# Four-tile column groups, sine tables on ScalarE and GpSimd roots in a two-part transformer kernel

## The chip, the cores and the metric

One core of a Trainium2 chip runs the whole program. The metric is device microseconds from start to end of one execution; lower is better. The kernel before takes 1556.37 us, the median of three runs (1552.61 to 1558.96).

## What is computed

A trunk of two layers works on 256 tokens and 256 context tokens of width 1024. Each layer has an attention branch (MLA), a pooling branch and a gated linear attention branch (GLA), which are gated, merged, multiplied with an output matrix, normalised and added to the stream. A second block follows: an RWKV-7 branch and a diagonal state-space branch (S5) in parallel, merged in the same way, and a gated feed-forward part. The lines that matter here, cut:

```python
def rmsnorm(x, g):
    y = xf * lax.rsqrt(jnp.mean(xf * xf, axis=-1, keepdims=True) + NORM_EPS)
...
def s5_branch(u, ...):
    a_bar = jnp.exp(lam * dt)                 # lam complex: modulus and phase
    bu = einsum('gpc,blgc->blgp', b_bar, ug)
    _, states = associative_scan(s5_combine, (a_elems, bu), axis=1)
    y = real(einsum('gcp,blgp->blgc', c, states)) + d * ug
...
def gla_inputs(zz, af_w2, af_b, ab_w2, ab_b):
    log_a_f = log_sigmoid(zz['gla_af'] @ af_w2 + af_b) / GLA_TAU
```

## The kernel before, in words

Activations lie with channels on the 128 partitions and tokens along the columns. SBUF holds an arena of 62 slots of 128x512 float32 (`S.get`, `S.put`; the oldest free slot is given out first). Weights come as units of 1 MB on SyncE's queue into raw tiles; `split` (L424, L426) makes a rounded high part on ScalarE and a low part on VectorE, or on GpSimd for each fourth one, and `mm3` (L441) does three matmuls per block of weights. A compile-time scheduler orders each engine's instructions by the order in which the program is written, as far as its own model finds them ready; on the chip each engine then runs its list in order. `weave` alternates the steps of a chain with those of a filler.

`rsqrt` (L488 to L496) computes a reciprocal root of a 128 x n tile in nine VectorE instructions: a first guess by integer arithmetic and two refinements. n is 2 at the boundaries between stages, 4 in `mla_prep`, 2 or 4 at the end of a GLA head, and 16 in two places of RWKV. `bcast` (L468) spreads the n columns over the partitions by TensorE transposes. `boundary` takes two roots in sequence: `r` normalises the output that has just been collected, and the root of `new` (L565) normalises the updated stream, of which `enter` then builds the next stage's input. For each of the eight channel tiles `update_x` adds the output to the stream, on GpSimd (L649, L650) or on VectorE (L653, L654, issued behind the second root), and `build_h` (L634 and the lines after it) makes high and low parts; the first matmuls of the next stage (`pen`) follow tile by tile.

`s5_prepare` runs woven with the third branch merge of layer 0. It computes sine and cosine of 32 phases per state row on ScalarE, and then, for each of 16 tiles, a table of 256 cosines and 256 sines by the addition theorem: six GpSimd products and sums (L1443 to L1448), stored to DRAM on SyncE's queue. In this stage `lo_every` keeps the low parts of the weights off GpSimd. `s5_chain` later loads a table per tile i, forms the inputs (`bu`, L1575), turns them (L1578 to L1581), scans (`recur`), and `output(i)` multiplies with C: four float32 matmuls of 32 columns of weights by 256 columns, which add up in rows 32(i mod 4) of one PSUM bank (L1559, tile `py`; two hardware records each).

`gla_decay` makes four gate matmuls with 32 rows of weights (L1026). The RWKV chain works in 64x64 quadrants: `sc`/`scl` (L1759, L1761), `pw` (L1815: eight heads of the upper half, then eight of the lower), `prh` (L1834: four of one half, then four of the other), `pmn` (L1849, L1850), `pyo` (L1856, L1857). `pQ`, `pY` and `pX` alternate the halves already.

Of the kernel before, what the change touches and what calls it, by code (L numbers as in the profile page):

```python
# [18 lines left out]
P = 128  # L19
L = 256  # L20
D = 1024
# [10 lines left out]
MOD_AT = (0, 1, 4)  # L32
S5_EARLY = (7, 5)
# [52 lines left out]
def _constants():  # L86
# [25 lines left out]
    c.add("iota", np.broadcast_to(np.concatenate([16.0 * np.arange(16), np.arange(16)]).astype(np.float32), (P, 32)))  # L112
    c.add("zero", np.zeros((P, 1), np.float32))
# [57 lines left out]
def _win_cols(w, name, t):  # L171
    if name == "misc":
        kr = w[:, OFF["kr"]:OFF["kr"] + 32]
        z = np.zeros((D, 32), w.dtype)
        return np.concatenate([kr, kr[:, ROPE_PERM], w[:, OFF["af"]:OFF["af"] + 32], z], 1)
    o = OFF[name] + P * t
    return w[:, o:o + P]
# [112 lines left out]
def gate_weights(inp, l):  # L290

    gw = np.zeros((32, 4, 2, 64), np.float32)
    gw[:16, :, 0] = np.asarray(inp["gla_af_w2"][l]).reshape(16, 4, 64)
    gw[16:, :, 1] = np.asarray(inp["gla_ab_w2"][l]).reshape(16, 4, 64)
    return _pad_rows(gw.reshape(32, 512), 64)
# [63 lines left out]
class B:  # L359
# [122 lines left out]
    def rsqrt(self, m, n):  # L482

        nc = self.nc
        r = self.sm.tile([P, 16], F32, tag="r", name="r")[:, :n]
        t = self.sm.tile([P, 16], F32, tag="t", name="t")[:, :n]
# [9 lines left out]
        self.chain_end = nc.vector.scalar_tensor_tensor(r, u, -0.9375, r, ALU.add, ALU.mult)  # L496
# [147 lines left out]
def update_x(b, k, st, xs, s_, pr, rs, on_pool):  # L644
# [26 lines left out]
def trunk(b, l, xs, st, A):  # L671
# [23 lines left out]
    if st is None:  # L695
# [13 lines left out]
        pr2 = b.bcast(b.rsqrt(A, 4), 4, b.pb)  # L709
# [312 lines left out]
    def gla_decay():  # L1022
        es = []
        for hd in range(4):
            ps = b.pa.tile([P, 512], F32, tag="p", name="pgate")
            nc.tensor.matmul(ps, gw[64:96, hd * P:(hd + 1) * P], misc[64:96], start=True, stop=True)  # L1026
# [324 lines left out]
def s5_prepare(b):  # L1351
# [29 lines left out]
    sn, cs = S.get(), S.get()  # L1381
    for t, ph in ((sn, 0.0), (cs, 0.25)):
        if ph:
            nc.vector.tensor_scalar(m, m, ph, None, ALU.add)
        nc.vector.tensor_scalar(r, m, MAGIC, -MAGIC, ALU.add, ALU.add)
        nc.vector.tensor_sub(t, m, r)
    zero = b.after((sn, cs), 0.0)
    for t in (sn, cs):
        nc.scalar.activation(t, t, AF.Sin, bias=zero, scale=6.283184)
    S.put(m, r)  # L1390
    yield
    sn3, cs3 = (t.rearrange("p (a c) -> p a c", c=32) for t in (sn, cs))

    s1, c1 = sn3[:, :, 17], cs3[:, :, 17]
# [40 lines left out]
    ring = [(S.get(), S.get()) for _ in range(2)]  # L1435
    for i in range(16):
        tab, tp = ring[i % 2]
        a3 = lambda t: t.rearrange("p (a c) -> p a c", c=16)
        can = cs[:, i * 32:i * 32 + 16].unsqueeze(2).broadcast_to((P, 16, 16))
        san = sn[:, i * 32:i * 32 + 16].unsqueeze(2).broadcast_to((P, 16, 16))  # L1440
        cbn = cs[:, i * 32 + 16:i * 32 + 32].unsqueeze(1).broadcast_to((P, 16, 16))
        sbn = sn[:, i * 32 + 16:i * 32 + 32].unsqueeze(1).broadcast_to((P, 16, 16))
# [8 lines left out]
        b.s5["tab"].append(d)  # L1451
        yield
    S.put(sn, cs, *ring[0], *ring[1])


def second_block(b, xs, st, A):
# [74 lines left out]
    def s5_chain():  # L1531
# [20 lines left out]
        def output(i):  # L1552
            _, t1, t2 = parts[i]
            rows, cc_ = slice(32 * (i % 4), 32 * (i % 4) + 32), slice(32 * i, 32 * i + 32)
            if i % 4 == 0:
                pys.append(b.pb.tile([P, 512], F32, tag="p", name="py5"))
            for n, (w_, x_) in enumerate(((cre, t1[:, 0:256]), (cren, t1[:, 256:512]), (cimn, t2[:, 0:256]),
                                          (cimn, t2[:, 256:512]))):
                nc.tensor.matmul(pys[-1][rows, C], w_[:, cc_], x_, start=n == 0, stop=n == 3)  # L1559
            S.put(t1, t2)  # L1560
# [4 lines left out]

        for i in range(16):
# [18 lines left out]
            if i > 1:  # L1585
                output(i - 2)
            yield
        recur(15)
        output(14)
        output(15)  # L1590
# [38 lines left out]
    def rwkv_chain():  # L1629
# [32 lines left out]
        rn = b.rsqrt(m16, 16)  # L1662
# [83 lines left out]
        for bt in range(2):  # L1746
            Lm, Y, X_ = S.get(), S.get(), S.get()
            for hd in range(4 * bt, 4 * bt + 4):
# [5 lines left out]
                for cc in range(2):  # L1754
                    for cp in range(2):
                        t0 = cc * P + cp * CH
                        orow = slice(cp * CH, cp * CH + CH)
                        for n, src in enumerate((BT, KT)):
                            nc.tensor.matmul(ps[orow, cc * 256 + n * P:cc * 256 + n * P + P].rearrange("p (a t) -> p a t", a=2),  # L1759
# [349 lines left out]
```

## Time and profile before

| | us |
|---|---|
| median of three runs | 1556.37 |
| the profiled execution | 1556.99 |
| its span, first to last instruction | 1555.2 |
| TensorE busy | 1435.6 |
| VectorE busy | 1101.0 |
| ScalarE busy | 688.8 |
| GpSimd busy | 491.1 |

The mean granted TensorE clock is 0.954 of full speed. A busy TensorE counts the latency of each matmul, so it is not TensorE at its peak: how close matmuls start to each other is read from the number of records in a stretch.

### The profile page before, as it was taken

The numbers are of one execution on the slowest core, as the hardware profiler recorded it, in microseconds if no ns is written. First come the engines' busy times: TensorE is split into PE (matmuls) and PEld (weight loads), VectorE is DVE, ScalarE is ACT, GpSimd is POOL, SyncE is SP. The second block draws the span as 40 slices with busy tenths as digits, with TensorE's granted clock in tenths as the row PEclk, the third lists the DMA queues.
The fourth block names the chain that finished last, engine by engine and source line by source line (L and its number), as shares of the span: only waits on it lengthen the run. The fifth ranks groups of instructions, "written<-read, shape, count | busy, mean of one in ns | idle before, by whom it ended". The sixth has DMA issues, their size and how long they took to land. (4 is left out here: it accounts for less than half of the span.)

```text
span 1555.2 us, 27544 instructions
## 1 busy us (share of the span) xinstructions
PE 1435.6 (92%) x10700; PEld 1216.2 (78%) x10700; DVE 1101.0 (71%) x2215; ACT 688.8 (44%) x1279; POOL 491.1 (32%) x503
## 2 busy tenths in 40 slices
PE   5999999998999999899998889979899999699996
PEld 1676776876788878886877789968668999699996
DVE  4565567887779555865579977768988549798843
ACT  3434445443433334454554455633532435376642
POOL 1000003354336954510035331334543003421212
PEclk8999999999999999899989999979999999799998
DMA  9534431321224253334024236734231325266560
GB/s 355 192 106 155 127 128 33 94 66 55 67 88 124 82 209 103 96 109 163 14 82 122 77 115 177 258 127 129 78 95 37 95 64 169 69 196 185 177 189 28
DMA packets 61043, 187.92 MB, mean 121 GB/s; under 512 B 7024, under 2 KB 8560, under 8 KB 60912
## 3 DMA queue, kind: packets, MB, share of 16 engines
q1 hardware_dynamic: 60912, 186.16, 38.2%
q8 instruction: 84, 1.38, 0.4%
q14 instruction: 47, 0.39, 0.1%
HBM read 180.10 MB, written 6.03 MB: 120 GB/s over the span
## 5 line engine op out<-in xcount | busy, mean ns | idle before, releaser
L424 ACT CAST wh<-raw 128x1024 fp32r<-128x1024 f32 (+1 forms) x296 | 279.5, 949 | 281.0 <-PE y L441 55.7
L426 DVE TENSOR_TENSOR wl<-raw,wh 128x1024 fp32r<-128x1024 f32 (+1 forms) x225 | 266.2, 1185 | 170.0 <-ACT wh L424 166.6
L426 POOL TENSOR_TENSOR wl<-raw,wh 128x1024 fp32r<-128x1024 f32 (+1 forms) x71 | 144.7, 2038 | 616.1 <-ACT wh L424 584.1
L441 PE MATMUL z_merge<-s,wh 128*128 128x512 f32 (+1 forms) x768 | 200.6, 351 | 1.8 <-ACT s L939 1.8
L441 PEld LDWEIGHTS z_merge<-s,wh 128*128 128x128 f32 x768 | 136.1, 198 | 19.7 <-ACT s L939 2.4
L441 PE MATMUL z_merge<-s,wl 128*128 128x512 f32 (+1 forms) x384 | 133.6, 348 | 0.3 <-DVE wl L426 0.2
L441 PE MATMUL pbr<-s,wh 128*128 128x256 f32 (+1 forms) x512 | 120.1, 326 | 0.8 <-DVE s L432 0.7
L441 PE MATMUL pup<-s,wh 128*128 128x256 f32 x656 | 118.5, 283 | 0.1
L441 PEld LDWEIGHTS pup<-s,wh 128*128 128x128 f32 x656 | 102.5, 192 | 0.2 <-ACT wh L424 0.2
L441 PE MATMUL y<-s,wh 128*128 128x256 f32 x496 | 98.1, 294 | 0.0
L441 PE MATMUL pwo<-s,wh 128*128 128x256 f32 (+1 forms) x448 | 94.1, 307 | 3.8 <-ACT s L1247 3.1
L441 PEld LDWEIGHTS pbr<-s,wh 128*128 128x128 f32 x512 | 86.8, 192 | 9.8 <-DVE s L432 1.0
L441 PE MATMUL pup<-s,wl 128*128 128x256 f32 x328 | 92.8, 283 | 0.0
L441 PEld LDWEIGHTS y<-s,wh 128*128 128x128 f32 x496 | 78.6, 193 | 7.8 <-issue 4.8
L441 PEld LDWEIGHTS z_merge<-s,wl 128*128 128x128 f32 x384 | 76.1, 198 | 9.5 <-DVE wl L426 1.1
L441 PE MATMUL pbr<-s,wl 128*128 128x256 f32 (+1 forms) x256 | 83.1, 325 | 0.0
L441 PEld LDWEIGHTS pwo<-s,wh 128*128 128x128 f32 x448 | 75.0, 199 | 7.7 <-ACT s L1247 3.7
L1134 ACT ACTIVATE s<-s 128x512 f32<-128x512 f32 (+1 forms) x64 | 33.2, 523 | 89.9 <-DVE s L1133 75.2
L441 PE MATMUL y<-s,wl 128*128 128x256 f32 x248 | 71.3, 287 | 0.0
L441 PE MATMUL pwo<-s,wl 128*128 128x256 f32 (+1 forms) x224 | 68.4, 306 | 1.5 <-DVE wl L426 1.5
L431 ACT CAST s<-s 128x256 fp32r<-128x256 f32 (+1 forms) x88 | 42.6, 488 | 60.7 <-DVE s L1204 17.9
L441 PE MATMUL pdn<-s,wh 128*128 128x256 f32 x352 | 63.4, 283 | 0.0
(480 smaller groups left out, 3618.8 us busy)
## 6 DMA issues: line engine op xcount, KB each, us to landing
raw<-wts SPq DMA_DIRECT2D x294, 512.0 KB, 4.4
s<-wts SPq DMA_DIRECT2D x57, 256.0 KB, 5.4
s5t<-s SPq DMA_DIRECT2D x16, 256.0 KB, 2.0
s<-s5t SPq DMA_DIRECT2D x16, 256.0 KB, 3.2
s<-xc SPq DMA_DIRECT2D x8, 256.0 KB, 5.0
x<-xc SPq DMA_DIRECT2D x8, 256.0 KB, 5.1
s<-tabs SPq DMA_DIRECT2D x4, 256.0 KB, 4.5
out<-s SPq DMA_DIRECT2D x8, 128.0 KB, 1.8
```

Of the source, the lines that this page charges most:

```text
L424: self.nc.scalar.copy(hi[:, :n], src)
L426: self.last_lo = eng.tensor_sub(lo[:, :n], src, hi[:, :n])
L431: self.nc.scalar.copy(hi, src)
L441: self.nc.tensor.matmul(ps, u, v[:, cols], start=start and n == 0, stop=stop and n == last)
L1134: nc.scalar.activation(E[:, lo:], E[:, lo:], AF.Exp, scale=1.0 / TAU)
```

## The change

1. `rsqrt` becomes one GpSimd instruction, the power -0.5, in 21 of 24 places; the first root of the program (n = 4) and the two roots of 16 columns keep the nine VectorE steps (`steps=True`). `update_x`'s GpSimd part is now the one that is issued behind the second root, and VectorE's part is free.
2. The 16 tables are made of phases: VectorE adds two phases (two additions of 256 columns), rounds (512 columns) and subtracts (512 columns); after each fourth tile ScalarE takes four sines of 512 columns, and four stores follow. `lo_every` and `NSLOT` stay.
3. `output` takes groups of tiles, 4, 4, 2, 2, 2 and 2, and goes round the group's column groups with each of the four terms. The group (0 to 3) is issued at step 5, the next at step 9, the pairs at 11, 13, 15 and the end; the slots of its products are held until then.
4. `gla_decay` issues its four gate matmuls as two pairs on different groups of 32 rows, and the weights are laid out twice for that. In RWKV, `sc`, `pw`, `prh`, `pmn` and `pyo` alternate halves from one matmul to the next.

```diff
-    def rsqrt(self, m, n):
+    def rsqrt(self, m, n, steps=False):
...
+        if not steps:
+            self.chain_end = nc.gpsimd.tensor_tensor(r, m, self.c("mhalf")[:, :n], ALU.pow)
+            return r
...
     if on_pool:
-        nc.gpsimd.tensor_mul(o_.ap, o_.ap, rs.ap)
-        nc.gpsimd.tensor_add(xs[s_][k], xs[s_][k], o_.ap)
+        with b.tc.issue_after(b.chain_end.ins):
+            nc.gpsimd.tensor_mul(o_.ap, o_.ap, rs.ap)
+            nc.gpsimd.tensor_add(xs[s_][k], xs[s_][k], o_.ap)
     else:
-        with b.tc.issue_after(b.chain_end.ins):
-            nc.vector.tensor_mul(o_.ap, o_.ap, pr[:, 0:256])
-            nc.vector.tensor_add(xs[s_][k], xs[s_][k], o_.ap)
+        nc.vector.tensor_mul(o_.ap, o_.ap, pr[:, 0:256])
+        nc.vector.tensor_add(xs[s_][k], xs[s_][k], o_.ap)
...
         for hd in range(4):
-            ps = b.pa.tile([P, 512], F32, tag="p", name="pgate")
-            nc.tensor.matmul(ps, gw[64:96, hd * P:(hd + 1) * P], misc[64:96], start=True, stop=True)
+            if hd % 2 == 0:
+                pgs = [b.pa.tile([P, 512], F32, tag="p", name="pgate") for _ in range(2)]
+                for i, ps in enumerate(pgs):
+                    rr = slice(64 + 32 * i, 96 + 32 * i)
+                    nc.tensor.matmul(ps, gw[rr, (hd + i) * P:(hd + i + 1) * P], misc[rr], start=True, stop=True)
+            ps = pgs[hd % 2]
...
     for i in range(16):
-        nc.gpsimd.tensor_tensor(a3(tab[:, 0:256]), can, cbn, ALU.mult)
-        nc.gpsimd.tensor_tensor(a3(tp[:, 0:256]), san, sbn, ALU.mult)
-        nc.gpsimd.tensor_tensor(a3(tab[:, 256:512]), san, cbn, ALU.mult)
-        nc.gpsimd.tensor_tensor(a3(tp[:, 256:512]), can, sbn, ALU.mult)
-        nc.gpsimd.tensor_sub(tab[:, 0:256], tab[:, 0:256], tp[:, 0:256])
-        nc.gpsimd.tensor_add(tab[:, 256:512], tab[:, 256:512], tp[:, 256:512])
-        d = b.tc.dram_tile([P, 512], F32, name=f"s5t{i}")
-        nc.sync.dma_start(d, tab)
+        for e in range(2):
+            am = mc[:, 256 * (1 - e) + 16 * i:256 * (1 - e) + 16 * i + 16].unsqueeze(2).broadcast_to((P, 16, 16))
+            bm = m3[:, i, 16:32].unsqueeze(1).broadcast_to((P, 16, 16))
+            nc.vector.tensor_tensor(t4[:, e], am, bm, ALU.add)
+        nc.vector.tensor_scalar(rd, tab, MAGIC, -MAGIC, ALU.add, ALU.add)
+        nc.vector.tensor_sub(tab, tab, rd)
+        if i % 4 == 3:
+            zero = b.after(tabs, 0.0)
+            for j, t in enumerate(tabs):
+                nc.scalar.activation(t, t, AF.Sin, bias=zero, scale=6.283184)
+                d = b.tc.dram_tile([P, 512], F32, name=f"s5t{i - 3 + j}")
+                nc.sync.dma_start(d, t)
...
-        def output(i):
+        def output(group):
+            for n, (w_, k, e) in enumerate(((cre, 1, 0), (cren, 1, 1), (cimn, 2, 0), (cimn, 2, 1))):
+                for i in group:
+                    rows, cc_ = slice(32 * (i % 4), 32 * (i % 4) + 32), slice(32 * i, 32 * i + 32)
+                    nc.tensor.matmul(pys[-1][rows, C], w_[:, cc_], parts[i][k][:, 256 * e:256 * e + 256],
+                                     start=n == 0, stop=n == 3)
...
-            if i > 1:
-                output(i - 2)
+            if i - 2 == groups[0][-1]:
+                output(groups.popleft())
...
-            for cp in range(2):
-                rr = slice(cp * CH, cp * CH + CH)
-                for hd in range(8):
+            for hd in range(8):
+                for cp in range(2):
+                    rr = slice(cp * CH, cp * CH + CH)
```

## Rows read from the trace of the kernel before

**Rows 1.** The page's first part: busy us, share of the span, instructions of each engine.

```profile
PE 1435.6 (92%) x10700; PEld 1216.2 (78%) x10700; DVE 1101.0 (71%) x2215; ACT 688.8 (44%) x1279; POOL 491.1 (32%) x503
```

**Rows 2.** Busy time by stretch; each line's columns: PE, PEld, DVE, ACT, POOL, PEclk, DMA, GB/s.

```profile
500.00:576.00 76.00, 73.98 (x316) 59.84 (x315) 43.44 (x47) 24.48 (x36) 62.00 (x76) 0.98 0.37 121
...
1047.00:1091.00 44.00, 41.40 (x284) 34.64 (x282) 37.18 (x58) 16.57 (x26) 19.91 (x15) 0.92 0.47 146
1091.00:1142.00 51.00, 46.09 (x315) 34.55 (x315) 48.09 (x74) 27.62 (x52) 33.57 (x31) 0.93 0.24 71
...
1168.00:1213.00 45.00, 44.78 (x840) 37.26 (x837) 36.90 (x57) 10.21 (x20) 15.37 (x14) 1.00 0.15 41
...
1227.00:1270.00 43.00, 43.00 (x613) 40.05 (x611) 16.11 (x45) 14.71 (x35) 2.58 (x2) 1.00 0.31 92
...
1331.00:1349.00 18.00, 7.11 (x29) 6.20 (x30) 11.93 (x38) 2.21 (x6) 8.45 (x13) 0.55 0.25 79
```

**Rows 3.** Groups of instructions: count, busy us, mean ns, idle before and its releasers.

```profile
L468 PE MATMUL ps_rb<-cons,r 128*128 128x128 f32 x60 | 12.9, 318 | 23.2 <-DVE r L496 23.2
...
L494 DVE TENSOR_SCALAR u<-t 128x2 f32<-128x2 f32 (+2 forms) x24 | 8.8, 366 | 0.7
...
L489 DVE TENSOR_TENSOR t<-r 128x2 f32<-128x2 f32 (+2 forms) x24 | 4.5, 187 | 0.5
```

**Rows 4.** Timeline, boundary ahead of the feed-forward part: start, duration, operation, [idle before <-releaser].

```profile
1339.91 0.16 DVE L561 TENSOR_TENSOR bs<-ps_ss,part 128x4 f32<-128x4 f32 x1 [1.69 <-PE ps_ss L460]
...
1341.94 0.16 DVE L565 TENSOR_TENSOR bA<-bA,bt 128x2 f32<-128x2 f32 x1
...
1342.61 0.72 POOL L649 TENSOR_TENSOR s<-s 128x256 f32<-128x256 f32 x1 [9.11 <-ACT s L662]
...
1343.39 0.65 DVE L492 TENSOR_TENSOR t<-r 128x2 f32<-128x2 f32 x1
...
1346.90 0.66 PE L468 MATMUL ps_rb<-cons,r 128*128 128x128 f32 x2 [4.77 <-DVE r L496]
1347.68 0.87 DVE L634 SCALAR_TENSOR_TENSOR s<-x,vec_b,ps_rb 128x256 f32<-128x256 f32 x2 [0.26 <-PE ps_rb L468]
...
1348.65 0.58 PE L441 MATMUL pen<-s,wh 128*128 128x256 f32 x1 [1.09 <-ACT s L636]
```

**Rows 5.** Groups of GpSimd's instructions by shape, one of the smallest and the largest.

```profile
L426 POOL TENSOR_TENSOR wl<-raw,wh 128x1024 fp32r<-128x1024 f32 x44 | 109.0, 2478 | 450.9 <-ACT wh L424 433.5 <-DMA x<-xc 17.3
...
L978 POOL TENSOR_TENSOR s<-s,cons 128x4 f32<-128x4 f32 x2 | 0.4, 202 | 0.1
```

**Rows 6.** Timeline of matmuls: start, duration of the whole batch, count; and one load group.

```profile
242.71 1.98 PE L1026 MATMUL pgate<-s,s 32*128 32x512 f32 x4
...
702.18 1.92 PE L605 MATMUL pmod<-raw,sc 128*32 128x512 f32 x16
...
1190.78 1.15 PE L1792 MATMUL pY<-s,s 64*64 64x64 f32 x32
...
1192.79 1.91 PE L1559 MATMUL py<-s,s 128*32 128x256 f32 x8
...
1226.44 1.85 PE L1815 MATMUL pw<-s,s 64*64 64x64 f32 x32
...
L1559 PEld LDWEIGHTS py<-s,s 128*32 128x32 f32 x128 | 13.5, 118 | 15.5 <-issue 5.4 <-POOL s L1581 0.7 <-DVE s L1764 0.6
```

**Rows 7.** Timeline around the phase tables, and the longest wait behind a load, 500 to 576.

```profile
467.08 0.43 DVE L1377 TENSOR_SCALAR s<-s 128x512 f32<-128x512 f32 x1
467.55 0.69 DVE L1378 TENSOR_TENSOR s<-s,s 128x512 f32<-128x512 f32 x1
...
472.72 1.28 ACT L1389 ACT_TABLE_LOAD   x1
...
584.95 0.42 DVE L519 TENSOR_TENSOR s<-s,s 128x256 f32<-128x256 f32 x1
...
ACT wh L424 <- DMA raw<-wts: 24.6, 6, 7.3
```

More of the change, by code (lines that the diff above doesn't have):

```diff
@@ L32 @@
 MOD_AT = (0, 1, 4)
+S5_GROUPS = ((4, 0), (4, 4), (2, 8), (2, 10), (2, 12), (2, 14))
 S5_EARLY = (7, 5)
@@ L112, in _constants @@
     c.add("iota", np.broadcast_to(np.concatenate([16.0 * np.arange(16), np.arange(16)]).astype(np.float32), (P, 32)))
+    c.add("mhalf", np.full((P, 16), -0.5, np.float32))
     c.add("zero", np.zeros((P, 1), np.float32))
@@ L708, in trunk @@
         nc.vector.tensor_scalar(A, ps[:, :4], EPS, None, ALU.add)
-        pr2 = b.bcast(b.rsqrt(A, 4), 4, b.pb)
+        pr2 = b.bcast(b.rsqrt(A, 4, True), 4, b.pb)
     if st:
@@ L1380, in s5_prepare @@
     nc.vector.tensor_add(m, m, r)
[L1381 to L1388, printed above, removed]
+    nc.vector.tensor_scalar(r, m, MAGIC, -MAGIC, ALU.add, ALU.add)
+    nc.vector.tensor_sub(m, m, r)
+    S.put(r)
+    mc = S.get()
+    s1, c1 = sm("s1"), sm("c1")
+    nc.vector.tensor_copy(s1, m3[:, :, 17])
+    nc.vector.tensor_scalar(c1, s1, 0.25, None, ALU.add)
+    nc.vector.tensor_scalar(k, c1, MAGIC, -MAGIC, ALU.add, ALU.add)
+    nc.vector.tensor_sub(c1, c1, k)
+    zero = b.after((s1, c1), 0.0)
+    for t in (s1, c1):
         nc.scalar.activation(t, t, AF.Sin, bias=zero, scale=6.283184)
-    S.put(m, r)
     yield
-    sn3, cs3 = (t.rearrange("p (a c) -> p a c", c=32) for t in (sn, cs))
-    s1, c1 = sn3[:, :, 17], cs3[:, :, 17]
     ur, ui, n2, kr, ki = sm("ur"), sm("ui"), sm("n2"), sm("kr"), sm("ki")
@@ L1550, in recur @@
             S.put(g5, tab)
-        def output(i):
-            _, t1, t2 = parts[i]
-            rows, cc_ = slice(32 * (i % 4), 32 * (i % 4) + 32), slice(32 * i, 32 * i + 32)
-            if i % 4 == 0:
+        def output(group):
+            if group[0] % 4 == 0:
                 pys.append(b.pb.tile([P, 512], F32, tag="p", name="py5"))
[L1557 to L1560, printed above, removed]
+            for n, (w_, k, e) in enumerate(((cre, 1, 0), (cren, 1, 1), (cimn, 2, 0), (cimn, 2, 1))):
[3 more added lines that the diff above has]
+                                     start=n == 0, stop=n == 3)
+            for i in group:
+                S.put(*parts[i][1:])
+            i = group[-1]
             if i % 4 == 3:
@@ L1564, in output @@
                 nc.scalar.activation(u_.ap, u_.ap, AF.Gelu_apprx_tanh)
+        groups = deque(range(o, o + n) for n, o in S5_GROUPS)
         for i in range(16):
@@ L1584, in s5_chain @@
                 recur(i - 1)
-            if i > 1:
-                output(i - 2)
+            if i - 2 == groups[0][-1]:
+                output(groups.popleft())
             yield
         recur(15)
-        output(14)
-        output(15)
+        for g in groups:
+            output(g)
         S.put(*s5w, sbr, sbi)
@@ L1661, in rwkv_chain @@
         nc.vector.tensor_scalar(m16, nk[:, 0:16], 1e-24, None, ALU.max)
-        rn = b.rsqrt(m16, 16)
+        rn = b.rsqrt(m16, 16, True)
         rnk = b.sm.tile([P, 16], F32, tag="rnk", name="rnk")
@@ L1754, in rwkv_chain @@
                 for cc in range(2):
+                    for n, src in enumerate((BT, KT)):
+                        for cp in range(2):
+                            t0 = cc * P + cp * CH
+                            orow = slice(cp * CH, cp * CH + CH)
+                            nc.tensor.matmul(ps[orow, cc * 256 + n * P:cc * 256 + n * P + P].rearrange("p (a t) -> p a t", a=2),
+                                             src[q].ap[rows, t0:t0 + CH], ar3[rows, :, t0:t0 + CH], start=True, stop=True)
                     for cp in range(2):
@@ L1829, in rwkv_chain @@
             if c:
-                for e in range(2):
-                    rows = slice(64 * e, 64 * e + 64)
-                    prh = b.pa.tile([P, 512], F32, tag="p", name="prh")
-                    for q in range(4):
+                prhs = [b.pa.tile([P, 512], F32, tag="p", name="prh") for _ in range(2)]
+                for q in range(4):
+                    for e, prh in enumerate(prhs):
+                        rows = slice(64 * e, 64 * e + 64)
                         nc.tensor.matmul(prh[rr, q * 64:q * 64 + 64], AR[q][rows, t0:t0 + CH], M[rows, q * 64:q * 64 + 64],
                                          start=True, stop=True)
+                for e, prh in enumerate(prhs):
                     nc.vector.tensor_add(w4[rr, :, e], w4[rr, :, e], prh[rr, 0:256].rearrange("p (q i) -> p q i", i=64))
@@ L1893, in rwkv_chain @@
         nc.vector.tensor_scalar(m16, nk[:, 0:16], 1.0 / 64, 64e-5, ALU.mult, ALU.add)
-        rn = b.rsqrt(m16, 16)
+        rn = b.rsqrt(m16, 16, True)
         rnk = b.sm.tile([P, 16], F32, tag="rnk", name="rnk2")
```

58 lines of the change are left out of this document (31 added, 27 removed).

## The prediction, made before the changed kernel ran

> **What bounds the kernel now.** I read the busy times first: TensorE 92% of the span, VectorE 71%, ScalarE 44%, GpSimd 32% [rows 1]. So most stretches end when TensorE's list ends, and an edit pays where it shortens TensorE's list or a wait ahead of it. The table of stretches [rows 2] sorts the places that the change touches. In 500 to 576 (tables woven into the merge) TensorE is busy 73.98 of 76 us, VectorE 43.44 and GpSimd 62.00: TensorE bounds, and VectorE has 32.6 us to spare. In 1047 to 1091 TensorE leads VectorE by 41.40 to 37.18 of 44. In 1091 to 1142 VectorE leads, 48.09 of 51. In 1168 to 1213 and 1227 to 1270 TensorE is busy to the last 0.2 us. In 1331 to 1349 it is busy 7.11 of 18 at a granted clock of 0.55, which is near the lower of its two levels (1.2 of 2.4 GHz): nothing bounds there but a chain of short steps. Third, the groups of instructions [rows 3]: before `ps_rb` TensorE stands idle 23.2 us, all for the last line of `rsqrt`. That is the largest wait that the change attacks. Its nine lines lie between 0.187 and 0.366 us each, some 0.27 in the mean, so 24 roots occupy VectorE for about 24 x 9 x 0.27 = 58 us. Last, the timeline of a boundary [rows 4], the one place where each step of the chain is seen.
>
> **1. Roots on GpSimd.** At the boundary [rows 4] L561 runs at 1339.91, three small operations and L565 follow until 1342.10, with the end of the first root between them; the second root then takes until 1346.8, because each small operation that takes 0.16 us alone takes 0.65 from the moment GpSimd starts to update x (L649 at 1342.61). `ps_rb` follows at 1346.90, `build_h` (L634) at 1347.68, the first `pen` at 1348.65. With the change the first root no longer lies on VectorE, so four operations of 0.2 us after L561 end at 1340.9. Then come a hop between engines, the power, and a hop back. A hop is 0.1 to 0.2 (L634 begins 0.1 after `ps_rb` ends). The power's price is in no row: GpSimd's smallest product takes 0.202 us, its slowest instruction 2.48 [rows 5]. I take 0.7, what it needs for a product of 256 columns (L649, 0.72): a power is more work than a product, but on two columns. So `ps_rb` starts at about 1341.9, five us earlier. The x update on GpSimd now stands behind the power: two instructions of 0.72 end at about 1343.1, L634 can run at 1343.2 instead of 1347.68, `pen` at about 1344.2. VectorE's part of the update is free before that, in the time in which it now waits. That is 4.4 us, twice (the other boundary, ahead of the second block, is alike): -9.
>
> Of the 23.2 us these two places hold 4.8 each; some 13.7 are left for the other roots, the entry's (unchanged) among them. An undisturbed root takes nine steps of about 0.2 us = 1.8 us, and the power with its hops 1.0, so a little under half of the 13.7 can go: -5. In the GLA heads the root's wait is covered by other TensorE work, and what counts is VectorE's time: 21 roots x 2.4 = 50 us less in all, most of it where VectorE is not the bound; -3. Sum -17. Bounds: with a power of 0.2 us and all of the 13.7 gone, -27; with one of 2.48 us, 1.8 us more on each exposed root. The exposed roots are 23.2 / 1.8 = 13, so +23 and the term is +6. A power also queues behind a low part of weights on GpSimd (L426, up to 2.48 us), which this bound covers, and the x update waits behind it in the same way.
>
> **2. S5 outputs.** One tile's output takes 1.91 us of TensorE, 16 of them 30.6 [rows 6]. `pmod` shows four column groups at work: 16 records of 512 columns in 1.92 us, which is as many columns as the 32 records of 256 of a group of four tiles. At that rate a group of four saves 3 x 1.91 = 5.7 us and a pair 1.9; two groups and four pairs 19 us. But a group of four also needs 32 loads of weights of 0.118 us [rows 6], 3.8 us if they go one after the other; then it saves 3.9, and the sum is 15.4. `pmod` cannot tell, since four loads (0.47) are as long as one of its steps (0.48). I take 17 us of TensorE. What of it counts: the three pairs within 1168 to 1226, 5.7 us, where TensorE bounds, I take 4; the group at step 5 in 1047 to 1091, where VectorE is close behind (4.2 us below), 2; in 1091 to 1168, where VectorE bounds, 1. Term -7, bounds -15 (nearly all) and +2 (the eight slots that a group of four holds make one transfer of a table wait, about one tile's 1.9 us).
>
> The load group and `pmod` [rows 6] are also where a rule can be weighed: 16 records with their loads in 1.92 us leave no room for 16 x 0.118 us of loads outside the matmuls. The Trainium skill ("TensorE: Matmul & The Clock Gate", Part 3, The mechanism) says that a weight load overlaps matmuls in flight only when its row group differs, which four full-height column groups never fulfil; by that rule the loads would stand outside, a group of four would take 1.9 + 3.8 us and save only 1.9, and the term would be about -4, the sum 1531. The trace of `pmod` disagrees, so I keep -7.
>
> **3. Quadrants and gates.** `pw` takes 1.85 us for 32 records one half after the other, `pY` with alternating halves 1.15 [rows 6]: 0.7 saved, twice, and as much again for the three `prh`, in a stretch with TensorE at 43.00 of 43 [rows 2]: -2.5. `pgate` shows 1.98 us for two matmuls (four records) [rows 6]; four in each of two layers make 8 us, pairs side by side would save 4, and as TensorE waits for VectorE in part of the GLA heads I take -1.5. For `sc`, `pmn` and `pyo`, neighbours already lie in different quadrants in part: 0. Term -4, bounds -6 and -1.
>
> **4. Tables.** VectorE gets per tile two additions of 256 columns (0.42 each, L519), a rounding (0.43) and a subtraction (0.69) [rows 7]: 1.96 us, 31 for 16 tiles, and some 4 for copies and the new angles, against 32.6 us idle [rows 2]. On paper it is 2.4 us too much; for it speaks that GpSimd's 62 us, beside which VectorE's operations grow (0.16 to 0.65 in [rows 4]), go away. ScalarE gets 16 sines of 512 columns, at its mean there of 24.48 / 36 = 0.68 us some 11 us, and, for a change of function before and after each of four batches, up to eight table loads of 1.28 us (10 us) [rows 7]; it is idle for 51.5 us [rows 2]. The stores on SyncE's queue, behind which weights wait (six waits for raw tiles, the longest 7.3 us [rows 7]), now wait for ScalarE in batches of four instead of GpSimd. TensorE has only 2.0 us idle there, so the gain can't exceed that: -1, bounds -2 and +10 (the overrun of 2.4 us and one wait like the longest).
>
> **Sum.** -17 - 7 - 4 - 1 = -29 us. The profiled execution took 1556.99 us, 0.6 above the median of the runs, so 1557 - 29 = **1528**. A measurement of this kernel can tell some 0.5%, 8 us, from no change.
>
> **Rivals.**
> - *The power costs as much as GpSimd's slowest instruction, about 2.5 us.* 13 exposed roots x 1.8 us take back 23: about 1551. For it: GpSimd has no power in this trace, and its time for 1024 columns shows that it is not quick; against it: two columns only. Chance 0.13.
> - *The other side: the power costs about 5 us.* One mechanism, at the 13 exposed roots: each us above 0.7 costs 13 us, and from 0.7 + 29/13 = 2.9 us on the kernel is slower than before. At 5 us, 13 x 4.3 = 56: about 1584. No row is that long. Chance 0.08.
> - *VectorE becomes the bound of the table stage.* 43.44 + 35 us in 76 leave nothing for the merge's own order; +10 to the term, 11 less gained: about 1539. For it the sum above, against it the room that GpSimd's contention gives back. Chance 0.12.
> - *The column groups don't run side by side* with these operands (the change doesn't do what it says): term 2 is nothing, about 1535. Against it `pmod`. Chance 0.09.
>
> The forecast keeps 0.58. The two last rivals lie within 0.5 to 2% faster; of the first, 1551, two thirds falls within 0.5% and the rest is faster. Faster 0.83, same 0.09, slower 0.08. **Range.** Low end: roots -25, outputs -12, quadrants -6, tables -2 and some luck in the queues, about 1510, I take 1508; high end: the 2.5 us power, 1552. Outside lie the 5 us power and a tenth for both tails.
>
> **What would show it.** `ps_rb` waits for a GpSimd row of about 0.7 us, and their sum falls from 23.2 to under 12; if it does not, step 1 is wrong, and the power's own row says whether by its size. The small operations between L561 and L565 no longer reach 0.65; `pen` starts about 4.4 us sooner after L561. `py` has batches of 32 records in 2 to 3.8 us (which of the two bounds, columns or loads, stands there); at 7.6 they don't run side by side. `pw` falls to about 1.15. In the table stage VectorE is busy about 75 of 76 us and TensorE's idle stays near 2 us; above 5 us, step 4 is wrong. The prediction as a whole fails if the power is longer than 2.9 us, or if TensorE's waits behind VectorE grow in stages where it now bounds.

## The result: 1539.5 us, and the profile after

The changed kernel took 1539.54 us, the median of four runs (1538.14 to 1543.14), beside 1557.45 for the kernel before on the same chip: a ratio of 0.9894, interval 0.9865 to 0.9923. Measured once more, beside the first experiments, it took 1535.31 beside 1554.99 (0.9874, 0.9856 to 0.9893). So the change gained 18 to 20 us, where 29 were forecast. The experiments are read against the second figure, the control; they ran in three rounds on three chips, on which the kernel before took 1554.99, 1554.67 and 1555.54 us.

The page of the changed kernel (span 1538.9 us) answers [rows 1]:

```profile
PE 1420.3 (92%) x10700; PEld 1217.1 (79%) x10700; DVE 1071.8 (70%) x2113; ACT 712.9 (46%) x1307; POOL 437.5 (28%) x428
```

VectorE gave up 29 us. Next the stretches that answer [rows 2], cut at the same work as before (tables; RWKV's 64x64 chain, from `pQ` to its end; `pw` to `pyo`; the boundary ahead of the feed-forward part). Columns as there: PE, PEld, DVE, ACT, POOL, then the granted clock.

```profile
501.00:577.00 76.00, 73.95 (x318) 60.49 (x317) 55.02 (x107) 51.05 (x65) 0.00 (x0) 0.98 0.49 159
1151.00:1217.00 66.00, 61.34 (x1112) 53.15 (x1110) 47.55 (x78) 17.85 (x35) 18.76 (x15) 0.95 0.14 42
1217.00:1258.00 41.00, 40.91 (x645) 38.30 (x641) 17.02 (x49) 15.71 (x38) 2.61 (x2) 1.00 0.33 103
1318.00:1334.00 16.00, 6.45 (x28) 5.88 (x28) 7.41 (x22) 2.38 (x6) 7.51 (x10) 0.58 0.33 96
```

The first and the third are as hoped. The second is the surprise: the same work as in 1167 to 1226 of the kernel before, there 59 us with TensorE busy for 58.6 of them at a granted clock of 1.00, here 66 with TensorE idle for almost 5 and a clock of 0.95. A gain of the earlier parts was given back in this place.

The groups of matmuls that answer [rows 3] and [rows 6] (count, busy us, mean ns, idle before and its releasers):

```profile
L471 PE MATMUL ps_rb<-cons,r 128*128 128x128 f32 x60 | 12.9, 317 | 13.9 <-POOL r L490 12.7 <-DVE r L502 1.1
...
L1579 PE MATMUL py<-s,s 128*32 128x256 f32 x128 | 12.4, 382 | 2.0 <-DVE s L1568 0.7 <-DVE s L1791 0.7 <-POOL s L1569 0.6
...
L1842 PE MATMUL pw<-s,s 64*64 64x64 f32 x64 | 2.2, 220 | 0.0
```

and GpSimd's powers, by form:

```profile
L490 POOL TENSOR_TENSOR r<-m,cons 128x4 f32<-128x4 f32 x7 | 10.1, 1441 | 55.2 <-DVE m L476 31.9 <-DVE ex_p L1353 12.2 <-ACT s L1098 11.1
L490 POOL TENSOR_TENSOR r<-m,cons 128x2 f32<-128x2 f32 x10 | 7.7, 774 | 40.2 <-DVE m L554 25.7 <-DVE m L476 9.9 <-DVE s L1145 4.5
L490 POOL TENSOR_TENSOR r<-bA,cons 128x2 f32<-128x2 f32 x4 | 3.2, 811 | 16.9 <-DVE bA L571 16.9
```

TensorE's idle time ahead of `ps_rb` fell from 23.2 to 13.9 us (under 12 was forecast), and nearly all of it now waits for the power. Two columns cost 0.77 to 0.81 us, four columns 1.44.

Where the time went is best read as stretches between matmuls with a name, from the list of each tile's matmuls (its first or last start). "1st" is the execution above, "2nd" that of the control.

| from - to, us | before | changed, 1st / 2nd | roots undone | single outputs | tables undone | 64 slots | before, 64 slots |
|---|---|---|---|---|---|---|---|
| first `z_q` - last `po` of layer 0 | 397.7 | 399.1 / 395.3 | 397.2 | 395.0 | 394.3 | 389.1 | 391.0 |
| - first `pwo` (tables) | 108.9 | 108.5 / 108.5 | 104.3 | 108.5 | 107.6 | 104.3 | 122.2 |
| - last `z_misc` (layer 1 entered) | 93.5 | 88.6 / 85.5 | 91.3 | 85.5 | 91.0 | 88.0 | 96.1 |
| - last `z_merge` | 318.6 | 311.5 / 311.4 | 317.1 | 312.5 | 312.5 | 306.8 | 309.2 |
| - first `pen` (boundary 1) | 42.6 | 41.2 / 41.3 | 43.2 | 40.5 | 40.5 | 40.5 | 42.6 |
| first `bu` - first `pQ` | 119.9 | 115.6 / 116.0 | 114.6 | 118.1 | 115.9 | 118.4 | 119.9 |
| - last `pY` | 59.1 | 66.4 / 66.1 | 66.4 | 59.1 | 66.1 | 58.8 | 59.7 |
| - last `pyo` | 40.9 | 37.4 / 37.4 | 37.4 | 37.4 | 37.4 | 37.4 | 40.9 |
| last `pwo` - first `pup` (boundary 2) | 19.9 | 17.7 / 17.7 | 19.8 | 17.4 | 17.7 | 17.3 | 19.9 |

How far a row can be trusted is shown by executions whose instruction lists are equal there. The first row spans 395.0 to 401.6 us among them, the third has two values, 85.5 and 88.6, and boundary 1 goes from 40.5 to 42.2. From the first `bu` to the first `pQ` two kernels with 64 slots and equal lists took 118.4 and 115.3 us. The two rows behind it and boundary 2 agree within 0.6 us. So 3 us say nothing in the first, the third and the `bu` row.

Part of this spread is TensorE's clock. The two executions of the changed kernel have the same lists and, where layer 1 is entered, the same waits, the longest of 2.8 us (`ps_sa`). The 84 matmul records from there on took this in the first and in the second:

```profile
633.00:650.00 17.00, 15.71 (x84) 15.42 (x84) 10.47 (x26) 3.84 (x9) 4.40 (x5) 0.60 0.51 161
...
628.00:642.00 14.00, 12.60 (x84) 12.31 (x84) 10.61 (x25) 4.08 (x9) 4.86 (x5) 0.76 0.57 179
```

The granted clock was 0.60 in one and 0.76 in the other, 3 us of difference. Laid matmul upon matmul, the first execution is 7.8 us behind the second by 647 us, and that distance changes by no more than 0.6 us from there to the first `bu`.

### The profile page after: what moved, and what is told of

Read it like the earlier page. It is cut to its first block, busy times and chain, and to the rows that moved or that the text cites. A ratio compares the mean times of both kernels' runs of the same rounds, so it can differ in the third digit from the quotient of the medians.

```text
span 1538.9 us, 27417 instructions
## 1 busy us (share of the span) xinstructions
PE 1420.3 (92%) x10700; PEld 1217.1 (79%) x10700; DVE 1071.8 (70%) x2113; ACT 712.9 (46%) x1307; POOL 437.5 (28%) x428
## 3 DMA queue, kind: packets, MB, share of 16 engines
q8 instruction: 84, 1.38, 0.4%
## 5 line engine op out<-in xcount | busy, mean ns | idle before, releaser
L444 PE MATMUL y<-s,wh 128*128 128x256 f32 x496 | 104.7, 308 | 1.0 <-DVE s L1546 1.0
L444 PEld LDWEIGHTS y<-s,wh 128*128 128x128 f32 x496 | 85.1, 209 | 5.3 <-issue 2.1
L444 PE MATMUL y<-s,wl 128*128 128x256 f32 x248 | 75.7, 305 | 0.0
L434 ACT CAST s<-s 128x256 fp32r<-128x256 f32 (+1 forms) x88 | 42.6, 487 | 60.0 <-DVE s L1216 14.3
```

Source lines behind the costliest of these rows:

```text
L434: self.nc.scalar.copy(hi, src)
L444: self.nc.tensor.matmul(ps, u, v[:, cols], start=start and n == 0, stop=stop and n == last)
```

## Experiments

Three questions were open. Theory **A** says that the roots gave about 10 us, that the groups of outputs cost some, and that the rest is small. **A1** and **A2** differ on why the groups cost: the slots that they hold, or the order of TensorE's list. **B** says that the power queues on GpSimd and loses what it wins. The control comes first, then each part of the change undone by itself, then the slots.

### The changed kernel again

> The changed kernel as it is, once more, beside the kernels that undo one part of it, so that each is read against it on the same chip. Every theory: 1539.5 us, within 3.

1535.31 us (1532.43 to 1539.81). The two measurements differ by 4 us, and the interval of one median is about 3 us to either side; differences below that are read from the stretches alone, in the rows that agree among equal lists.

### Roots undone

```diff
-        if not steps:
-            self.chain_end = nc.gpsimd.tensor_tensor(r, m, self.c("mhalf")[:, :n], ALU.pow)
-            return r
...
     if on_pool:
-        with b.tc.issue_after(b.chain_end.ins):
             nc.gpsimd.tensor_mul(o_.ap, o_.ap, rs.ap)
```

> The changed kernel with all 24 roots in nine VectorE steps again, and update_x ordered as before; outputs, quadrants, gates and tables stay changed. The prediction's step 1 says that the roots gave 17 us: 1556. Theory A, from the two traces, says that they gave about 10 (some 6 where layer 1 is entered, 2 at each of the two boundaries of the second block, little in layer 0): 1549. Theory B says that a power that queues behind low parts on GpSimd loses what it wins: 1541.

1547.32 us, ratio 0.9949 (0.9937 to 0.9962): the roots gave 12.0 us, near theory A and 5 below the prediction. B falls. By stretch, against the second run of the changed kernel: 5.8 us where layer 1 is entered (2.7 against the first run, whose clock was lower there), 5.7 in layer 1, 1.9 and 2.1 at the boundaries, 1.3 at the end; and 4.2 the other way in the table stretch. These 4.2 us have one place in the control, at 512 us, where TensorE waits for a cast of ScalarE:

```profile
PE pbr L444 <- ACT s L434: 1.8, 1, 1.8
```

ScalarE has put two sines of the new tables and a load of a function table (1.28 us) ahead of that cast. From 500 to 524 TensorE then ran 88 records at a granted clock of 0.93; with the roots undone ScalarE's list falls in another order, there is no wait, and 90 records take 20 us at 1.00. The changed kernel has no wait there with the old tables either, nor with 64 slots. So the 4.2 us are not the roots' own: they are paid for the tables' work on ScalarE, in an order that the roots helped to set.

### One power more

```diff
+            nc.gpsimd.tensor_tensor(r, m, self.c("mhalf")[:, :n], ALU.pow)
             self.chain_end = nc.gpsimd.tensor_tensor(r, m, self.c("mhalf")[:, :n], ALU.pow)
```

> The changed kernel with every one of the 21 powers computed twice in a row: it measures what one more us per root costs, on which the prediction's break-even of 2.9 us rests. The prediction: 13 exposed roots, 0.8 us each for two columns and 1.4 for four, so 10 to 13 us: 1546 to 1548. Theory A counts in the trace nine or ten places where TensorE stands idle for a power, 12.7 us in all, and adds 0.9 us at each: 8 to 9 us, 1544. Theory B, the powers mostly lie beside other work: 3 us, 1538.

1556.68 us, ratio 1.0003 (0.9990 to 1.0015): all of the change's gain is gone. The second powers, by form:

```profile
L491 POOL TENSOR_TENSOR r<-m,cons 128x4 f32<-128x4 f32 x7 | 8.4, 1194 | 0.6
...
L491 POOL TENSOR_TENSOR r<-m,cons 128x2 f32<-128x2 f32 x10 | 8.0, 800 | 0.8
...
L491 POOL TENSOR_TENSOR r<-bA,cons 128x2 f32<-128x2 f32 x4 | 2.8, 703 | 0.3
```

8.4 + 8.0 + 2.8 = 19.2 us more on GpSimd cost 1556.7 - 1535.3 = 21.4 us against the control. Every theory was too low: about as much is lost as is added, not at 13 of 21 places alone. How exactly is open. In the trace `ps_rb` waits 21.9 us for the power, 12 times, against 12.7 us, 9 times, so 9.2 us of the loss stand there in plain sight. Of the 24.2 us between the two profiled executions, 2.9 lie ahead of the first power and 2.2 between `bu` and `pQ`, where there is none; and beside the pairs below, a run of the same round, the loss is only 13.2 us. The break-even needs no such working: the 21 powers take 1.00 us in the mean (21.0 in all), with the second ones 1.91 us, and at that price the kernel is level with the one before (1.0003). So the power decides at about 1.9 us, not at 2.9.

### Four columns in steps again

The kernel of the section "64 slots and another order at the boundaries", further down, with:

```diff
-        if not steps:
+        if not steps and n < 4:
```

> The kernel of e10 with the power on GpSimd for two columns only; the seven roots of four columns take the nine VectorE steps again. A power of four columns takes 1.44 us in the changed kernel, of two 0.81. Theory A: 1.44 with two hops is as long as nine steps of 0.2, so nothing changes: within 3 us of e10. Rival, the queue of GpSimd in the layers makes these roots late: 4 to 6 us less than e10.

1515.80 us beside 1516.18 of that kernel: no difference. Within the 3 us that a median can tell, the power on four columns is worth as much as nine VectorE steps here. If that holds with 62 slots too, where it wasn't measured, the seven roots of four columns gave nothing, and the 14 of two columns gave the 12 us.

### Single outputs

```diff
-S5_GROUPS = ((4, 0), (4, 4), (2, 8), (2, 10), (2, 12), (2, 14))
+S5_GROUPS = tuple((1, i) for i in range(16))
```

> The changed kernel with S5's outputs one tile at a time, each two steps after its tile, as in the kernel before; all else stays changed. The prediction's step 2 says that the groups gave 7 us: 1546. Theory A says that TensorE's time was saved where TensorE waits for VectorE, and that the end of this stage is set by S5's chain, whose last tile came no sooner in the changed kernel: 1538 to 1541. Theory B says that the held slots and the later order cost: 1534 to 1537.

1532.68 us (0.9857, 0.9840 to 0.9875) beside 1535.31 (0.9874): no slower without the groups, and the stretch from the first `bu` to the last `pY` is 177.2 us beside 182.1. The groups themselves do what they say: a group of four runs its 32 records in the time that one tile took before, 1.91 us for eight (TensorE's timeline of the changed kernel):

```profile
1081.79 1.93 PE L1579 MATMUL py<-s,s 128*32 128x256 f32 x32
```

So the loads aren't what limits it (one after the other, 32 x 0.118 us would be 3.8); the forecast's upper rate holds. But TensorE's busy time fell where others set the pace. In the second part, from `pQ` on, where the prediction put 4 us of gain, the groups lose 7.0. In the first part they gain 2.1, which is within what equal lists differ there.

### Pairs only

```diff
+S5_GROUPS = tuple((2, i) for i in range(0, 16, 2))
```

> The changed kernel with eight pairs of S5 outputs in place of groups of 4, 4, 2, 2, 2 and 2. Theory A1 (held slots): the last four pairs are the same and hold the same, the first eight tiles hold four slots less; the stretch from the first bu to the last pY takes about 180 us. Theory A2 (order of TensorE's list): pairs fill the waits in the first half again, the second half keeps its 7 us loss: 179 to 180. Rival B, the groups of four alone cost: 177. The time: 1533 by either A, 1530 by B.

1543.47 us (0.9921, 0.9899 to 0.9942). The time says little: its profiled run was already 8.6 us behind the control's at the last `po` of layer 0, and up to 1052 us the lists are the same. That is a warning for the other comparisons of two medians, too. The stretches say more: 116.2 and 66.5 us, as with the groups of four. So the groups of four aren't needed for the loss; what both kernels share is the last four pairs.

### 64 slots

```diff
-NSLOT = 62
+NSLOT = 64
```

> The changed kernel with 64 slots in place of 62. Theory A1: S5's groups cost 5 us between the first bu and the last pY (182 us against 177 with single outputs) because the slots that a group holds make a producer wait for a slot, as a multiplication of RWKV's chain waits for S5's last GpSimd product in the trace; two more slots give back 2 to 4 us of it: 1531 to 1533, and that stretch 178 to 180 us. Theory A2: it is the order of TensorE's list, whose single outputs filled its waits for VectorE and whose groups leave 24 us idle there instead of 9; slots change nothing: 1535, and 181 to 182 us.

1516.24 us, ratio 0.9759 (0.9739 to 0.9779): 19 us less than the control, where A1 had expected 2 to 4. The stretch from `pQ` to the last `pY` is 58.8 us, with the same groups, TensorE busy nearly all along and the clock at 1.00:

```profile
1134.00:1193.00 59.00, 58.21 (x1138) 50.97 (x1134) 48.73 (x78) 18.43 (x36) 16.50 (x15) 1.00 0.17 49
```

So the slot count is the cause of the 7 us. A2 falls: TensorE's list in this stretch is the same in both kernels but for the first few records. What the run doesn't separate is the wait for a slot from the order of VectorE's list, which the scheduler also changed with the slots (20 of 77 instructions of this stretch stand elsewhere). The rest lies in layer 0 (6.2), in the table stretch (4.2), in layer 1 (4.6) and at the boundaries (1.2), less 2.5 where layer 1 is entered and 2.4 from `bu` to `pQ`, which are no sure figures. The waits show how a slot costs. First VectorE's in the changed kernel, 1151 to 1217 (who waited for what: us, times, longest):

```profile
DVE s L1811 <- POOL s L1569: 2.3, 2, 1.2
DVE s L1567 <- PE pQ L1815: 2.2, 1, 2.2
```

L1811 multiplies two of RWKV's tiles into a fresh slot, L1569 is a product of S5; neither reads the other's data. What L1811 can wait for is its slot: by the program it is given the oldest free one, here one that L1569 still reads (`g5` or `tab`, put back by `recur`). S5's scan L1567 writes into a fresh slot in turn, which the `pQ` matmuls still read. The timeline of one such knot:

```profile
1168.55 1.79 POOL L1569 TENSOR_TENSOR s<-s,s 128x512 f32<-128x512 f32 x1 [0.63 <-DVE s L1567]
...
1170.37 0.69 DVE L1811 TENSOR_TENSOR s<-s,s 128x512 f32<-128x512 f32 x1 [1.18 <-POOL s L1569]
...
1171.74 1.26 POOL L429 TENSOR_TENSOR wl<-raw,wh 128x512 fp32r<-128x512 f32 x1 [1.40 <-DVE s L1824]
1172.18 1.38 DVE L1811 TENSOR_TENSOR s<-s,s 128x512 f32<-128x512 f32 x1
...
1173.70 1.97 PE L1815 MATMUL pQ<-s,s 64*64 64x64 f32 x32 [2.63 <-DVE s L1811]
...
1175.71 0.69 DVE L1567 TENSOR_TENSOR_SCAN s<-s_rho,s 128x256 f32<-128x256 f32 x1 [2.16 <-PE pQ L1815]
```

VectorE's list stands 1.2 us at the first L1811. The L1811 that `pQ` needs is a later one (1172.18), which takes 1.38 us instead of 0.69 beside a low part on GpSimd, and `pQ` waits 2.6 us for it; then the other branch's scan waits for `pQ`. The pause is paid a second time in the clock: this `pQ` takes 1.97 us, where others take 1.10, and the granted clock of 1165 to 1184 is 0.82. Over the whole stretch TensorE is idle for 3.9 us more than with 64 slots and busy for 3.1 us more with about the same work. With 64 slots L1811 waits for another instruction, and shorter, and the scan no longer for `pQ`; the same view, 1134 to 1193:

```profile
DVE s L1811 <- PE py L1579: 0.9, 1, 0.9
DVE s L1567 <- POOL s L1569: 0.6, 1, 0.6
```

### 64 slots, single outputs

> The changed kernel with 64 slots and S5's outputs one tile at a time. It measures the groups where no slot is short. The prediction's step 2 says that groups are worth 7 us: 1523 beside 1516. Theory A: VectorE sets the end of this stage, and TensorE's 17 us less are worth nothing: 1516, and 177 us from the first bu to the last pY as with the groups. Rival: the groups cost by their later order even so: 1512.

1522.87 us (0.9787, 0.9766 to 0.9808) beside 1516.24 (0.9759, 0.9739 to 0.9779): 6.6 us, near the prediction's 7, but the intervals overlap, and the stretch in which the two kernels differ, first `bu` to last `pY`, is 177.7 against 177.2 us. Up to 1034 us the lists of the two kernels are equal, so the 2.2 us at `pwo` in layer 0 and the 0.9 in layer 1 by which their executions differ are not of the groups. Two more kernels with groups and 64 slots, and with the same list in this stretch, took 174.3 and 175.2 us there (those of "64 slots and another order at the boundaries" and of "Four columns in steps again"). So where slots suffice the groups are worth 0.4 to 3.4 us by this stretch, and 6.6 by the time; which of these holds is open.

### The kernel before with 64 slots

> The kernel before with 64 slots in place of 62, nothing else. 64 slots made the changed kernel 19 us faster, 7 of it between the first pQ and the last pY, 12 in the layers and the table stage, where the change holds no more slots than before. Theory A: those 12 were there in the kernel before too, the 7 were not: 1543 beside 1555, and 59 us from the first pQ to the last pY as with 62. Rival: the change made the slots scarce everywhere: 1554.

1559.35 us, ratio 1.0026 (1.0013 to 1.0038): no gain at all. The time fits the rival; the stretches don't. Layer 0 took 6.7 us less and layer 1 9.4 less, so slots were short there too before the change, as theory A has it; and 13.3 us of that were lost again in the table stretch, 2.6 behind it. TensorE's waits in 457 to 581 come to 14.2 us, against 2.0 in this stage with 62 slots. The longest of them:

```profile
538.39 9.39 DVE L426 TENSOR_TENSOR wl<-raw,wh 128x1024 fp32r<-128x1024 f32 x1 [14.38 <-ACT wh L424]
...
545.98 0.72 POOL L1448 TENSOR_TENSOR s<-s,s 128x256 f32<-128x256 f32 x1
...
547.84 0.79 PE L441 MATMUL z_merge<-s,wl 128*128 128x512 f32 x1 [8.20 <-DVE wl L426]
```

A low part on VectorE, otherwise 1.2 to 1.5 us long here, took 9.39 us. It began while GpSimd was making tables, one instruction straight behind the other; GpSimd's last one ended at 546.70, and the low part ended 1.1 us after that. TensorE waited 8.2 us for it. No other VectorE instruction in any of the traces is longer than 3.5 us. GpSimd, the fifth column of the table of stretches, had been busy all of the time:

```profile
500.00:540.00 40.00, 36.43 (x160) 29.53 (x158) 18.29 (x19) 10.01 (x15) 40.00 (x54) 1.00 0.31 105
```

Of the other waits 2.8 us belong to a root, and 3.2 us come from SyncE's queue, which stands at stores of tables that GpSimd hasn't finished, so that a weight behind them reaches ScalarE 14.4 us late (waits of SyncE's queue, 500 to 581, and of ScalarE, 457 to 581):

```profile
SPq L1450 <- POOL s L1448: 40.1, 11, 5.3
...
ACT wh L424 <- DMA raw<-wts: 14.4, 1, 14.4
```

The standing of the queue alone doesn't make the loss: in 470 to 590 it stands 54.9 us at these stores here and 64.6 with 62 slots, where TensorE hardly waits. What differs is which work meets it, since the slots also change the order of the lists.

The new tables take GpSimd's work away, and the changed kernel with 64 slots has no wait of TensorE in this stage (104.3 against 122.2 us). So by the traces the new tables are worth little with 62 slots and much with 64. A run with 64 slots and the old tables beside the rest of the change, which would show it, was not made.

### Tables undone

> The changed kernel with the 16 tables made by GpSimd's six products and sums again; roots, outputs, quadrants and gates stay changed. The prediction's step 4 says 1 us: 1540.5. Theory A, from the two traces, says that the stage gained 0.4 us of its own, and that what follows it is the roots': 1540. Rival, VectorE became the bound of the stage and the tables cost 10 us: 1530.

The edit puts the old loop of the 16 tables and its ring of slots back. 1538.76 us (0.9910, 0.9886 to 0.9933) beside 1535.31: 3.4 us in favour of the change, within the intervals. TensorE's list is the same in both kernels, so the traces can be laid matmul upon matmul. The old tables win 4.3 us up to 520, which is the wait for ScalarE's cast described at the roots, and lose 8.8 from there to 620, so the new ones are ahead by 4.5; four other runs with the new tables keep their distance to the control from 440 to 620. The rival that VectorE becomes the bound falls: VectorE is busy 55.0 of 76 us, not 75. In this stretch the additions, roundings and subtractions for the tables take 21.1 us (some of the 16 tables are made ahead of it), and other work of VectorE got shorter with GpSimd silent. VectorE's groups in this stage of the kernel before (483 to 576):

```profile
L426 DVE TENSOR_TENSOR wl<-raw,wh 128x1024 fp32r<-128x1024 f32 (+1 forms) x19 | 23.5, 1236 | 25.9 <-ACT wh L424 25.9
...
L1204 DVE SCALAR_TENSOR_TENSOR s<-s,s 128x512 f32<-128x512 f32 x4 | 4.3, 1084 | 0.1
```

and the same in the changed kernel (485 to 577):

```profile
L429 DVE TENSOR_TENSOR wl<-raw,wh 128x1024 fp32r<-128x1024 f32 (+1 forms) x19 | 18.9, 995 | 12.7 <-ACT wh L427 12.4 <-DMA raw<-wts 0.3
...
L1216 DVE SCALAR_TENSOR_TENSOR s<-s,s 128x512 f32<-128x512 f32 x4 | 2.7, 678 | 0.0
```

### Quadrants and gates undone

> The changed kernel with pgate, sc, pw, prh, pmn and pyo in the order of the kernel before; roots, outputs and tables stay changed. The prediction's step 3 says 4 us: 1539 beside a changed kernel of 1535. Theory A reads the stretch from pw to the last pyo as 37.4 us in the changed kernel against 40.9 before and gives the gates nothing further: 3.5 us, 1538.8. Rival: the single outputs ran at 1532.7 and tables and roots make 16 of the 20 us, so 4 to 7 us are left for this part: up to 1542.

The edit puts the six orders of the kernel before back. 1543.24 us (0.9936, 0.9912 to 0.9960): 7.9 us, of which the stretch to the last `pyo` shows 3.5 (40.9 against 37.4). Laid matmul upon matmul against the control, layer 0's gates cost 0.9 (from `pgate` to the first `pbr` 4.3 against 3.4), but by 270 us that is made up again. In layer 1 the distance grows by 3.2 us between 766 and 865, where the two executions of the changed kernel move by 0.6 against each other; only 0.7 of it stand between `pgate` and `pbr`. The rest of the 7.9 is within the scatter of layer 0 and of the entry of layer 1. `pw` and `pgate` run as pairs (timeline of the changed kernel):

```profile
241.85 1.12 PE L1037 MATMUL pgate<-s,s 32*128 32x512 f32 x2
...
1217.48 1.10 PE L1842 MATMUL pw<-s,s 64*64 64x64 f32 x32
```

### 64 slots and another order at the boundaries

```diff
-        pr = self.bcast(r, n, self.pa)
...
         self.token_sums(ps, n, last[2], f=self.c("mean"))
+        pr = self.bcast(r, n, self.pa)
...
-(0, 1, 3, 5, 7)
+(2, 4, 6)
```

> The changed kernel with 64 slots, and at the boundaries the second sums ahead of the first root's spread on TensorE, and update_x of the tiles 0, 1, 3, 5 and 7 on VectorE, of 2, 4 and 6 on GpSimd. The prediction gave each of the two boundaries of the second block 4.4 us; the changed kernel gained about 2.2. Theory A: 1.0 us went to sums that stand behind the spread, 0.9 to two GpSimd products ahead of the first tile's sum; this brings both back, so the stretch from the last pwo to the first pup falls from 17.4 to about 15.5, the one from z_merge to pen by as much, and the time to 1512. Rival: VectorE, now with five tiles and all of build_h, becomes the chain: 17 us and 1516 or more.

1516.18 us beside 1516.24: no difference in time. The two boundary stretches fell by 1.0 each (39.5 and 16.3); the kernel of "Four columns in steps again", with the same boundaries, has 41.2 and 15.9, so only the second fall stands. In the changed kernel's boundary, the counterpart of [rows 4], one sees what the prediction missed:

```profile
1325.25 0.88 POOL L490 TENSOR_TENSOR r<-m,cons 128x2 f32<-128x2 f32 x1 [4.13 <-DVE m L554]
...
1326.19 0.69 PE L471 MATMUL ps_rb<-cons,r 128*128 128x128 f32 x2 [2.02 <-POOL r L490]
...
1326.67 1.71 PE L463 MATMUL ps_ss<-cons,s 128*128 128x1 f32 x8
...
1328.41 0.16 DVE L567 TENSOR_TENSOR bs<-ps_ss,part 128x4 f32<-128x4 f32 x1 [2.85 <-PE ps_ss L463]
...
1329.90 0.15 DVE L571 TENSOR_TENSOR bA<-bA,bt 128x2 f32<-128x2 f32 x1
...
1330.13 0.81 POOL L490 TENSOR_TENSOR r<-bA,cons 128x2 f32<-128x2 f32 x1 [3.99 <-DVE bA L571]
...
1330.99 0.69 PE L471 MATMUL ps_rb<-cons,r 128*128 128x128 f32 x2 [2.62 <-POOL r L490]
...
1333.15 0.48 DVE L640 SCALAR_TENSOR_TENSOR s<-x,vec_b,ps_rb 128x256 f32<-128x256 f32 x1 [1.98 <-POOL x L657]
...
1334.12 1.01 PE L444 MATMUL pen<-s,wh 128*128 128x256 f32 x3 [2.44 <-ACT s L642]
```

The second sums (1326.67) stand behind the first spread, which waits for a power; the small operations behind L567, to the end of L571, have VectorE's x updates between them and take 1.5 us instead of 0.8; and the first tile waits for three GpSimd operations, since two products are issued ahead of the first addition. The edit cured the last (L640 0.73 us behind `ps_rb` instead of 2.16). The first it did not touch: the scheduler put the sums behind the spread again, so what that order costs was not measured.

## Why the prediction was right in direction and too large

The time lies in the range, and faster was right; 29 us were forecast, 18 to 20 came. Undone one at a time, the parts are 12.0 + 7.9 + 3.4 - 2.6 = 20.7 us, beside 19.7 for the whole. Each of the four carries several us of scatter, so it is partly chance that they add up so closely. It is luck, too, that the sum missed by no more than ten: steps 1 and 2 together gave some 14 us less than forecast, and steps 3 and 4 some 6 more.

- **Step 1, -17; measured -12.** The mechanism was right: `ps_rb` waits for a GpSimd row of 0.8 us, and the 0.65 us operations are gone. The price was mis-sized for four columns: 0.7 for all roots, where four columns take 1.44 and, in the run that gave them their steps back, gained nothing. The sign that was named, a wait of under 12 us ahead of `ps_rb`, missed with 13.9. At the boundaries 4.4 us were forecast each, and 1.4 (42.6 to 41.2, with 40.5 to 42.2 among equal lists) and 2.2 (19.9 to 17.7) came, for the reasons above: the step followed one chain and not what the scheduler would put between its links. From L561's counterpart to the first `pen` the gain is 3.0 us (8.74 to 5.71), and part of it is lost ahead of L567, where the sums now stand behind the first spread. The 4.4 us were worked out with one product ahead of the first addition, where two stand. So the boundaries gave 4 us for the 9 forecast; the layers gave 11.5 for 8, of which 3 may be the clock's, and 4.2 were lost on ScalarE in the table stretch, which the step did not have.
- **Step 2, -7; measured +2.6 with 62 slots (by the stretch +4.9), between -0.4 and -6.6 with 64.** This is the step that failed, by more than any other. The rate was right, even at its upper end. Two things were wrong: that a stretch with TensorE busy 44.8 of 45 us [rows 2] is bound by TensorE alone (with the outputs in groups TensorE waits there for VectorE, 4.7 us idle in 66), and that holding eight slots costs at most one late table. The price of held slots was named, as the bound of +2, with the wrong victim: not S5's own table, but RWKV's `lk` product, which is written into the next free slot. By the prediction's last sign, TensorE's waits behind VectorE growing where TensorE bounds, it failed in this stage.
- **Step 3, -4; measured -3.5 in the stretch alone, -7.9 in the time.** `pw` fell to 1.10 as read from `pY`. The gates were read from their own row, which would give 0.9 and 0.7 us; in layer 1 the heads behind them came some 3 us sooner.
- **Step 4, -1; measured -3.4 in the time, -4.5 laid matmul upon matmul.** VectorE's load in the stretch rose by 11.6 us, not by 35: part of the tables lies ahead of it, and what shared the time with GpSimd got shorter (low parts 1.24 to 1.00 us). The forecast had this relief as an argument without a number. What it left out is ScalarE's order: the loads of function tables were priced against ScalarE's idle time, and yet one cast came late and cost 4 us. The queue of SyncE behind GpSimd, which the step named and didn't price, cost little (3.2 us of TensorE's time in the kernel before with 64 slots); GpSimd's hold on one VectorE instruction cost 8.2.
- **The rivals.** Powers of 2.5 or 5 us didn't come, but the point from which the power decides was about 1.9 us, not 2.9. The 13 exposed roots were a division (23.2 / 1.8), not a count: the trace has ten such waits, two of them 4.8 us long. And it took only waits on which TensorE stood still at `ps_rb`; in the run with two powers these grew by 9.2 us and the time by more, so a later root seems to push back other work too. Column groups do run side by side.
- **The weight loads.** The Trainium skill ("TensorE: Matmul & The Clock Gate", Part 3, The mechanism) lists a load as overlapping running matmuls only when its row group differs; the 32 records in 1.93 us of four full-height column groups disagree, as `pmod` had.

The best kernel seen is the changed one with 64 slots, 1516.2 us (0.9759 of before); the further edits (1516.2, 1515.8) add nothing that can be told from it.

## What to carry to other kernels

An edit that groups work holds its inputs longer. Before counting the time that it saves, count the buffers that it holds, and ask who takes the next free one: with a shared arena the wait turns up in a neighbour's chain, as a wait between two instructions that share no data. Two shortages can hide each other: neither 64 slots alone (+4 us) nor the change alone (-20) shows the 39 us that both give, so a spare buffer is worth a run on either side of a change. And before a difference between two runs is explained, compare two executions of one instruction list: here they were up to 8 us apart in their first 650 us.

## What had not been expected of the hardware

GpSimd's power took 0.77 to 0.81 us for 128x2 elements and 1.44 for 128x4 (0.70 to 0.80 and 1.19 for a second power straight behind the first), while a product of 128x256 on the same engine takes 0.72. With GpSimd busy 62 of 76 us, the 19 low parts of weights on VectorE in that stage took 1.24 us in the mean, and 1.00 with GpSimd idle; another operation of 128x512 elements 1.08 and 0.68. Where GpSimd ran product behind product without a gap, one low part begun among them took 9.39 us and ended 1.1 us after the last of them. With the same list and the same waits, TensorE's granted clock over the same 84 records was 0.60 in one execution and 0.76 in another.
